# One hybrid-decoder layer on one core: the tokens' own part computed in the scan's head, with the inverse's second product and with kappa

## The chip, the core and the metric

The kernel runs on one core of one Trainium2 chip. The core has a matrix engine (TensorE, PE in the profile; its weight loads are shown as PEld), VectorE (DVE), ScalarE (ACT), GpSimd (POOL) and a queue engine for DMAs (SyncE, SP). The time is device microseconds of one execution. The kernel before takes 1354.36 us, the median of three runs (1353.73 to 1357.92).

## What is computed

One inference step of one layer: RWKV-7 time mixing beside dilated sliding-window attention, gated and merged, for a prompt of 1024 tokens and 8 short samples. Only the RWKV part of the prompt matters here. Per head it is a recurrence over tokens on a 64x64 state S:

```python
def step(S, inp):
    r_t, w_t, k_t, v_t, kk_t, a_t = inp
    sa = jnp.einsum('bhvk,bhk->bhv', S, -kk_t)
    S = (S * w_t[:, :, None, :] + sa[..., None] * (kk_t * a_t)[:, :, None, :]
         + v_t[..., None] * k_t[:, :, None, :])
    return S, jnp.einsum('bhvk,bhk->bhv', S, r_t)

S_fin, o = lax.scan(step, wkv0.astype(F32), xs)
```

## The kernel before

The recurrence is done in chunks of 64 tokens. Inside a chunk the removal terms `sa` of the 64 tokens depend on each other through a triangular matrix; its inverse is needed. A *unit* is one pair of heads (j = 0..3) and one half of the prompt (hf = 0, 1): 8 units, each with 8 chunks. Five streams of work share the core in the first stage of the kernel, up to about 615 us:

- `products`: the input projection, 36 blocks of 128 columns in this stage (`project_steps`, line L178). One piece is four matmuls of 128x352, written to a bank `pj`. This is the bulk of PE's work and it can go between anything.
- `units` (generator `unit`): prepares a unit on DVE and ACT, with small matmuls: the normalisation (L326), the decay and rate gates (L306), the transpose of the norms (L349; after it on DVE the block L351, L353, L357, L359, L360 of 128x512 operations), the triangular products (L385) with their masks on DVE (L392, into `AT`), the bonus (L405), transposes of v (L413, into `W`) and of the keys (L423, into `BT`), and last **R0** (L432): 16 matmuls of 64x64 of `AT` and `W`, moved out of PSUM by ACT at L436. R0 is the tokens' own part: what the values of a chunk's own tokens give to its removal terms.
- `inverses` (`inverse`): two 32x32 blocks of each triangle are inverted on DVE by forward substitution, `tm` and `X` (L457, L460, 62 operations a unit), after a DMA to DRAM and back (`Yd`, `Y`); the result goes back to `AT` by DMA through `Xd` (L464).
- `scans` (`scan`): the scan of a unit. Its *head* joins the two 32x32 inverses into a 64x64 one: DMAs `AT<-Xd` and a transpose `T1` on DVE (L479), a transpose of kappa (L484), the first product `pm` (L492), the second product `pg` (L502), moved into `AT` by ACT (L508). Then kappa is multiplied by the inverse (L518, banks `pk`, moved into `KR` by ACT at L523), and R0 is multiplied by the inverse (L528, bank `pu`, moved back into `R0` by ACT at L532). Then 8 *hops*, one a chunk: `KR` with the state (L543), W on DVE (L544), `BT` with W (L549), the new state on DVE (L552). Last the outputs (L560).
- `norms` (`norm`): the group norm of a finished scan (DVE, ACT, and the transposes L589).

PE executes in the order in which the program is written; DVE, ACT and the queues are ordered by the framework's scheduler. The written order comes from a planner, `run_streams`: each stream yields a pair, the PE time of what it has just written and the delay after which its next step is due. Whenever a stream is due its step is written; otherwise a piece of projection is. `own` streams (scans and inverses) go ahead of the limit on small work, the others wait while more than `SMALL` of it is owed. PSUM banks go round by name: `sc` has two, `g` has two, `pj` has four.

Of the kernel before, what the change touches and what calls it, by code (L numbers as in the profile page):

```python
# [14 lines left out]
AF = mybir.ActivationFunctionType  # L15
# [3 lines left out]
P = 128  # L19
# [12 lines left out]
D_PN, D_KR, D_AT, D_G, D_W, D_INV, D_UP = 0.65, 1.81, 4.5, 0.2, 2.09, 1.3, 8.4  # L32
D_PM, D_HOP, D_ST, D_GN, D_IN, D_U0, D_MASK = 0.9, 1.25, 1.75, 12.6, 11.0, 1.2, 1.2
# [51 lines left out]
def tile_layer(ctx: ExitStack, tc: tile.TileContext, A: dict, O: list):  # L85
    nc = tc.nc
    V, S, G, T, SP = nc.vector, nc.scalar, nc.gpsimd, nc.tensor, nc.sync
# [29 lines left out]
    rp = rw_stack.enter_context(tc.tile_pool(name="rp", bufs=1))  # L117
# [199 lines left out]
    def unit(j, hf, M, st, out):  # L317
# [47 lines left out]
        E = mk(rp, [P, 8, 65], "E", 2)  # L365
# [3 lines left out]
        KR = mk(rp, [P, 4, 4, 64], "KR", 2)  # L369
# [8 lines left out]
        AT = mk(rp, [P, 2, 8, P], "AT", 2)  # L378
        for h in range(2):
            pA = [ps("g") for e in range(2)]  # L380
            for q in range(4):
                c = 4 * h + q
                for e in range(2):
# [5 lines left out]
                        start=True, stop=True,  # L389
# [13 lines left out]
        bon = t_("bon", 2)  # L403
# [6 lines left out]
        W = mk(rp, [P, 8, P], "W", 2)  # L410
# [7 lines left out]
        BT = mk(rp, [P, 8, P], "BT", 2)  # L418
        for h in range(2):
# [3 lines left out]
                T.transpose(pt[:, q * P : (q + 1) * P], BK[:, c // 2, 2 * (c % 2) : 2 * (c % 2) + 2, :], ident)  # L423
            S.activation(BT[:, 4 * h : 4 * h + 4, :], pt.rearrange("p (a b) -> p a b", a=4), AF.Copy)
            yield (0.45, D_W)
        R0 = mk(rp, [P, 4, P], "R0", 2)
        pr = ps("g")
        for c2 in range(4):
            for e in range(2):
                for p in range(2):  # L430
                    u, v = slice(64 * (1 - p), 64 * (1 - p) + 64), slice(64 * p, 64 * p + 64)
                    T.matmul(  # L432
                        pr[u, c2 * P + 64 * e : c2 * P + 64 * e + 64], AT[v, e, 2 * c2 + p, u], W[v, 2 * c2 + p, 64 * e : 64 * e + 64],
                        start=True, stop=True,
                    )
        S.activation(R0[:], pr.rearrange("p (a b) -> p a b", a=4), AF.Copy)  # L436
        yield (1.0, D_G)

        out.append((j, hf, KR, AT, W, BT, R0, E, bon, st))


    def inverse(j, hf, AT, out):
# [25 lines left out]
        out.append((Xd, blk))  # L468


    def scan(j, hf, KR, AT, W, BT, R0, E, bon, st, Xd, blk, out):

        T1 = mk(rp, [P, 8, 32], "T1", 1)
        quads = [(p, 64 * (1 - p), n, n // 4, 2 * (n % 4) + p) for p in range(2) for n in range(8)]
        for p in range(2):
            u = 64 * (1 - p)
# [5 lines left out]
        pk = ps("sc")  # L482
# [3 lines left out]
        for p in range(2):  # L486
            u, v = slice(64 * (1 - p), 64 * (1 - p) + 64), slice(64 * p, 64 * p + 64)
# [3 lines left out]
        for _, u, n, e, c in both:  # L491
            T.matmul(  # L492
                pm[u + 32 : u + 64, 32 * n : 32 * n + 32], AT[u : u + 32, e, c, u + 32 : u + 64], T1[u : u + 32, n, :],
                start=True, stop=True,
            )
        for p in range(2):
            u = 64 * (1 - p)
# [3 lines left out]
        for _, u, n, e, c in both:  # L501
            T.matmul(  # L502
                pg[u : u + 32, 32 * n : 32 * n + 32], T1[u + 32 : u + 64, n, :], AT[u + 32 : u + 64, e, c, u + 32 : u + 64],
                start=True, stop=True,
            )
        for p in range(2):
            u = 64 * (1 - p)
            S.activation(  # L508
                AT[u : u + 32, :, p::2, u + 32 : u + 64], pg[u : u + 32, 0:256].rearrange("p (a b c) -> p a b c", a=2, b=4), AF.Copy
            )  # L510
        yield (0.6, D_PM)


        chunks = [(c // 2, c % 2, e) for c2 in range(4) for e in range(2) for c in (2 * c2, 2 * c2 + 1)]
        pk = [ps("sc") for p in range(2)]
        for c2, p, e in chunks:
            u = slice(64 * (1 - p), 64 * (1 - p) + 64)
# [1 line left out]
                pk[p][64 * e : 64 * e + 64, 64 * c2 : 64 * c2 + 64],  # L519
                kT[u, c2, 64 * e : 64 * e + 64], AT[u, e, 2 * c2 + p, u], start=True, stop=True,  # L520
            )
        for p in range(2):
            S.activation(KR[:, :, 1 + p, :], pk[p][:, 0:256].rearrange("p (a b) -> p a b", a=4), AF.Copy, scale=-1.0)  # L523
        yield (1.0, D_PM)
        pu = ps("sc")
        for c2, p, e in chunks:
            u = slice(64 * (1 - p), 64 * (1 - p) + 64)
            T.matmul(  # L528
                pu[u, c2 * P + 64 * e : c2 * P + 64 * e + 64],
                AT[u, e, 2 * c2 + p, u], R0[u, c2, 64 * e : 64 * e + 64], start=True, stop=True,  # L530
            )
        S.activation(R0[:], pu.rearrange("p (a b) -> p a b", a=4), AF.Copy, scale=-1.0)  # L532
        yield (1.0, D_U0)

        Ot = mk(rp, [P, 4, P], "Ot", 2)
        for c in range(8):
            p, c2 = c % 2, c // 2
            u, v = slice(64 * (1 - p), 64 * (1 - p) + 64), slice(64 * p, 64 * p + 64)
# [3 lines left out]
            pr = ps("sc")  # L542
# [14 lines left out]
        for c in range(8):  # L557
            c2, v = c // 2, slice(64 * (c % 2), 64 * (c % 2) + 64)
# [39 lines left out]
    def state_out(j, st):  # L598
        b = ps("g")
        T.transpose(b[:, 0:P], st[0][:], ident)  # L600
        so = mk(rp, [P, P], "so", 1)
        S.activation(so[:], b[:, 0:P], AF.Copy)
        for e in range(2):
            d = slice(64 * e, 64 * e + 64)
            S.dma_start(O[8][0, 0, 2 * j + e], so[d, d])
# [878 lines left out]
```

## Time and profile before

| what | value |
|---|---|
| median of 3 runs | 1354.36 us |
| the profiled execution | 1353.07 us, of which the span from first to last instruction is 1351.2 us |
| PE busy | 1318.8 us, 98% of the span |
| DVE, ACT, POOL busy | 805.1, 469.3, 67.6 us |
| first stage, 76 to 600 us | 524 us, of which PE busy 510.26 us |
| R0 (L432) and its product with the inverse (L528) on PE | 9.2 us busy each, in 8 units |

PE's busy time counts overlapping matmuls once, and the end of a matmul is modelled, so a small idle time hides part of a loss. A better measure of what a group costs PE is the distance from its start to the start of the next group. In the timeline rows of the prediction the columns are the start in us, the time to the end of the row's last instruction, engine, line, operation, output and inputs, forms, count; a wait in brackets is idle time ahead of it with what ended it. fp32 matmuls stand twice in the profile's counts (32 for the 16 of R0).

### The profile page before, as it was taken

What the parts mean: (1) busy time and instruction counts of PE and PEld (TensorE: products, weight loads), DVE (VectorE), ACT (ScalarE), POOL (GpSimd) and SP (SyncE); (2) the same over time, 40 slices, a digit from 0 to 9 for tenths busy, and PEclk for the clock granted to TensorE, in tenths of its full rate; (3) what the DMA queues carried; (4) which work ended last, traced back from release to release, by engine and by line L of the source; (5) the groups of instructions that cost most, each with busy time, mean ns of one, the idle gap of its engine ahead of it and who ended that gap; (6) DMA issues with size and microseconds to landing.
All of it is one profiled execution on the core that took longest, in us unless ns stands there. A gap on an engine that the chain in (4) does not pass through costs nothing.

```text
span 1351.2 us, 25749 instructions
## 1 busy us (share of the span) xinstructions
PE 1318.8 (98%) x10005; PEld 1238.6 (92%) x10005; DVE 805.1 (60%) x2204; ACT 469.3 (35%) x1065; POOL 67.6 (5%) x82
## 2 busy tenths in 40 slices
PE   9999999999999999999999999999999998999997
PEld 7998999898988999999999999999999997899786
DVE  5677668686576856552554376437544744655565
ACT  5334344434344443422332333232333234132211
POOL 0000000000000000000000000000000000025100
PEclk9999999999999999999999999999999999999999
DMA  6122223222313242326646365545555566795221
GB/s 211 45 60 64 71 87 88 62 58 78 100 53 87 81 112 85 93 92 135 134 104 134 98 144 113 127 119 122 113 128 134 123 134 164 219 298 166 91 98 66
DMA packets 340151, 151.64 MB, mean 112 GB/s; under 512 B 188808, under 2 KB 329502, under 8 KB 339774
## 3 DMA queue, kind: packets, MB, share of 16 engines
q1 hardware_dynamic: 241150, 129.68, 35.3%
q10 hardware_dynamic: 98880, 20.32, 7.6%
q8 instruction: 79, 1.29, 0.4%
q14 instruction: 42, 0.34, 0.1%
HBM read 110.68 MB, written 38.97 MB: 111 GB/s over the span
## 4 chain that ended last, share of the span: by engine, by line
PE 82%; DVE 11%; DMA 3%; issue 1%; ACT 1%; SPq 0%; POOL 0%; ACTq 0%; DVEq 0%; POOLq 0%
PE pj L178 60%; PE pj L1438 7%; PE s L948 2%; PE o L985 2%; DMA kc<-in_cache_kv_g_dram 2%; DVE tm L457 2%; DVE X L460 2%; PE g L385 1%; PE t L968 1%; DVE st L552 1%; PE sc L543 1%; DVE wlo L169 1%; PE sc L549 1%; DMA cb<-yd 1%; PE sc L528 1%
## 5 line engine op out<-in xcount | busy, mean ns | idle before, releaser
L178 PE MATMUL pj<-xhi,whi 128*128 128x352 f32 x1848 | 396.4, 336 | 4.3 <-ACT xhi L1305 2.9
L178 PE MATMUL pj<-xhi,wlo 128*128 128x352 f32 x1848 | 385.7, 330 | 0.0
L178 PE MATMUL pj<-xlo,whi 128*128 128x352 f32 x1848 | 381.1, 327 | 0.0
L178 PEld LDWEIGHTS pj<-xhi,whi 128*128 128x128 f32 x1848 | 305.3, 190 | 14.4 <-issue 4.4
L178 PEld LDWEIGHTS pj<-xlo,whi 128*128 128x128 f32 x1848 | 309.4, 190 | 2.3 <-issue 1.3
L178 PEld LDWEIGHTS pj<-xhi,wlo 128*128 128x128 f32 x1848 | 307.8, 190 | 3.7 <-issue 1.9
L169 DVE TENSOR_TENSOR wlo<-wraw,whi 128x512 fp32r<-128x512 f32 x162 | 113.9, 704 | 74.4 <-ACT whi L168 73.9
L168 ACT ACTIVATE whi<-wraw 128x512 fp32r<-128x512 f32 x162 | 100.5, 625 | 117.1 <-PE pj L178 73.4
L958 ACT ACTIVATE Sm<-Sm,nm 128x128 f32<-128x128 f32 (+1 forms) x96 | 42.4, 442 | 88.4 <-DVE nm L955 88.4
L457 DVE TENSOR_TENSOR tm<-Y,X 128x60 f32<-128x60 f32 (+24 forms) x248 | 52.0, 210 | 10.7 <-DMA Y<-Yd 4.4
L950 DVE CUSTOM_DVE_ANT_0 Sm<-s,cst 128x128 f32<-128x128 f32 (+1 forms) x96 | 29.2, 347 | 45.5 <-PE s L948 45.4
L460 DVE TENSOR_TENSOR X<-X,tm 128x60 f32<-128x60 f32 (+24 forms) x248 | 51.8, 209 | 6.0
L552 DVE SCALAR_TENSOR_TENSOR st<-sc,E,SD 64x64 f32<-64x64 f32 x128 | 36.1, 282 | 29.5 <-PE sc L549 27.8
L1438 PE MATMUL pj<-wl,mh 128*128 128x512 f32 (+1 forms) x136 | 52.0, 382 | 0.0
L541 ACT ACTIVATE SD<-st,E 128x128 f32<-128x128 f32 x64 | 25.7, 401 | 70.9 <-DVE st L552 70.8
L811 POOL TENSOR_TENSOR kvp<-vv,kv 128x512 f32<-128x512 f32 x16 | 21.2, 1331 | 461.0 <-DVE Ss L819 376.5
L985 PE MATMUL o<-PT,Vt 128*128 128x128 f32 x280 | 38.6, 275 | 0.8 <-ACT PT L972 0.8
L985 PEld LDWEIGHTS o<-PT,Vt 128*128 128x128 f32 x280 | 36.6, 191 | 1.3 <-ACT PT L972 1.1
L948 PE MATMUL s<-k,q 128*128 128x128 f32 (+1 forms) x192 | 37.7, 325 | 0.1
L873 ACT ACTIVATE k<-pj 128x352 f32<-128x352 f32 (+1 forms) x36 | 16.3, 456 | 61.6 <-PE pj L178 56.8
L311 ACT ACTIVATE zt<-pj,der 128x352 f32<-128x352 f32 x48 | 26.5, 552 | 31.7 <-PE pj L178 26.4
L873 ACT ACTIVATE q<-pj 128x352 f32<-128x352 f32 (+1 forms) x36 | 16.4, 455 | 58.4 <-PE pj L178 54.6
(325 smaller groups left out, 1687.3 us busy)
## 6 DMA issues: line engine op xcount, KB each, us to landing
wraw<-in_w_in_dram SPq DMA_DIRECT2D x146, 256.0 KB
gd<-zt SPq DMA_DIRECT2D x48, 176.0 KB
gt<-gd SPq DMA_DIRECT2D x48, 176.0 KB
vs<-bt ACTq DMA_DIRECT2D x48, 128.0 KB
kc<-in_cache_kv_g_dram SPq DMA_DIRECT2D x48, 128.0 KB
Vt<-vs ACTq DMA_DIRECT2D x12, 512.0 KB
cb<-cd SPq DMA_DIRECT2D x12, 512.0 KB
zd<-zt SPq DMA_DIRECT2D x24, 176.0 KB
```

The costliest lines, as they stand in the source:

```text
L168: S.activation(hi[:], raw[:], AF.Copy)
L169: V.tensor_tensor(lo[:], raw[:], hi.bitcast(F32)[:], ALU.subtract)
L178: T.matmul(out, w[wi][:, n % 4, :], x[:, n % 4, :], start=first and n == 0, stop=last and n == 11)
L457: V.tensor_tensor(tm, Y[:, r : r + 1, r + 1 : 32].to_broadcast([P, m, n]), X[:, 0:m, r : r + 1].to_broadcast([P, m, n]), ALU.mult)
L460: V.tensor_tensor(X[:, 0:m, r + 1 : 32], X[:, 0:m, r + 1 : 32], tm, ALU.subtract)
L552: V.scalar_tensor_tensor(S1[d, d], pS[d, d], E[d, c, 64:65], SD[d, d], ALU.mult, ALU.add)
L873: S.activation(classes(dst[:], d)[:, :, t0 // d : (t0 + n) // d], b[:, 0:n].rearrange("p (i c) -> p c i", c=d), AF.Copy)
L948: T.matmul(r, qT[:, i * P : (i + 1) * P], kT[:, keys[i][0] * P : keys[i][0] * P + n], start=True, stop=True)
L950: V.tensor_tensor_reduce(out=Sm[:, i, 0:n], in0=r, in1=m3 if g == 2 else m12[:, 256 - n : 256], scale=1.0, scalar=NEG, op0=ALU.add, op1=AL ...
L958: S.activation(Sm[:, i, 0:n], Sm[:, i, 0:n], AF.Exp, scale=SCALE, bias=nm[:, x : x + 1], accum_out=ml[:, g, 1, i : i + 1])
L985: T.matmul(po[:, (i % 4) * P : (i % 4 + 1) * P], st["Vt"][:, kb_, :], PT[:, n * P : (n + 1) * P], start=m == 0, stop=m == len(keys[i]) - 1,)
L1438: T.matmul(pb[:], a[:, k], wk, start=x == 0, stop=x == len(prods) - 1)
```

## The change

R0's 16 matmuls leave `unit` and stand in `scan`, directly behind the second product `pg`; their bank is still a `g`. R0's eviction stands behind the two of `pg`. R0 has one buffer where it had two. The product of R0 with the inverse (`pu`) is written directly behind kappa's (`pk`), ahead of kappa's evictions, and its bank is a `g` where it was an `sc`. The planner is told 1.2 for `pg` with R0 (0.6 before), 1.7 for `pk` with `pu` (1.0 and 1.0 before, as two steps), and one step of 1.0 fewer in `unit`. No DMA moves, and the number of instructions that compute is the same.

```diff
@@ unit
-        R0 = mk(rp, [P, 4, P], "R0", 2)
-        pr = ps("g")
-        for c2 in range(4):
...
-        S.activation(R0[:], pr.rearrange("p (a b) -> p a b", a=4), AF.Copy)
-        yield (1.0, D_G)
@@ scan
+        R0 = mk(rp, [P, 4, P], "R0", 1)
+        pr = ps("g")
+        for c2 in range(4):
+            for e in range(2):
+                for p in range(2):
+                    u, v = slice(64 * (1 - p), 64 * (1 - p) + 64), slice(64 * p, 64 * p + 64)
+                    T.matmul(
+                        pr[u, c2 * P + 64 * e : c2 * P + 64 * e + 64], AT[v, e, 2 * c2 + p, u], W[v, 2 * c2 + p, 64 * e : 64 * e + 64],
+                        start=True, stop=True,
+                    )
         for p in range(2):
             u = 64 * (1 - p)
             S.activation(
                 AT[u : u + 32, :, p::2, u + 32 : u + 64], pg[u : u + 32, 0:256].rearrange("p (a b c) -> p a b c", a=2, b=4), AF.Copy
             )
-        yield (0.6, D_PM)
+        S.activation(R0[:], pr.rearrange("p (a b) -> p a b", a=4), AF.Copy)
+        yield (1.2, D_PM)
...
-        for p in range(2):
-            S.activation(KR[:, :, 1 + p, :], pk[p][:, 0:256].rearrange("p (a b) -> p a b", a=4), AF.Copy, scale=-1.0)
-        yield (1.0, D_PM)
-        pu = ps("sc")
+        pu = ps("g")
         for c2, p, e in chunks:
...
+        for p in range(2):
+            S.activation(KR[:, :, 1 + p, :], pk[p][:, 0:256].rearrange("p (a b) -> p a b", a=4), AF.Copy, scale=-1.0)
         S.activation(R0[:], pu.rearrange("p (a b) -> p a b", a=4), AF.Copy, scale=-1.0)
-        yield (1.0, D_U0)
+        yield (1.7, D_U0)
```

**Place 1, PE in the head of the second scan.** In the rows a name's number tells one tile from another; L178 is a piece of projection. Before, from the first product (L492) to the first of kappa's matmuls (L518):

```order
L492 MATMUL sc_2210<-T_391_2191,AT_1114 32x32 x16
L178 MATMUL pj_2025<-xlo_13_94,whi_2124 128x352 x4
L178 MATMUL pj_2238<-xhi_10_91,whi_2243 128x352 x4
L502 MATMUL sc_2251<-AT_1114,T_391_2191 32x32 x16
L178 MATMUL pj_2238<-xhi_10_91,wlo_2244 128x352 x4
L178 MATMUL pj_2238<-xlo_12_93,whi_2243 128x352 x4
L518 MATMUL sc_2278<-AT_1114,sz_2203 64x64
```

Before, from the last of kappa's matmuls to the first hop (L543):

```order
L518 MATMUL sc_2279<-AT_1114,sz_2203 64x64
L178 MATMUL pj_2239<-xhi_10_91,whi_2243 128x352 x4
L589 MATMUL g_2302<-ident_69,Ot_1574 128x128 x4
L528 MATMUL sc_2313<-R_237_1303,AT_1114 64x64 x16
L178 MATMUL pj_2239<-xhi_10_91,wlo_2244 128x352 x4
L178 MATMUL pj_2239<-xlo_12_93,whi_2243 128x352 x4
L405 MATMUL g_2340<-t_2104,cst_76 128x512
L543 MATMUL sc_2346<-st_67_385,KR_1053 128x128
```

Now the same two stretches (L479 is the first product, L489 the second, L500 is R0, L517 kappa, L524 `pu`, L541 the hop, L587 the norm's transposes):

```order
L479 MATMUL sc_2213<-T_391_2185,AT_1079 32x32 x16
L178 MATMUL pj_2200<-xhi_10_91,wlo_2206 128x352 x4
L178 MATMUL pj_2200<-xlo_12_93,whi_2205 128x352 x4
L489 MATMUL sc_2240<-AT_1079,T_391_2185 32x32 x16
L500 MATMUL g_2258<-W_1176,AT_1079 64x64 x16
L178 MATMUL pj_2201<-xhi_10_91,whi_2205 128x352 x4
L587 MATMUL g_2282<-ident_69,Ot_1569 128x128 x4
L517 MATMUL sc_2293<-AT_1079,sz_2197 64x64
```

```order
L517 MATMUL sc_2294<-AT_1079,sz_2197 64x64
L524 MATMUL g_2311<-R_402_2257,AT_1079 64x64 x16
L178 MATMUL pj_2201<-xhi_10_91,wlo_2206 128x352 x4
L178 MATMUL pj_2201<-xlo_12_93,whi_2205 128x352 x4
L178 MATMUL pj_2202<-xhi_10_91,whi_2205 128x352 x4
L541 MATMUL sc_2346<-st_67_385,KR_1024 128x128
```

R0 has joined the second product and `pu` has joined kappa, with no piece between; one piece and the norm's transposes stand between R0 and kappa.

**Place 2, DVE at the head of the first scan.** T1 is the transpose that the first product waits for (L479, now L466); the 128x512 rows at L351 to L360 prepare the third unit, and the rows at L242 to L253 shift a projected block `m`. Before:

```order
L351 SCALAR_TENSOR_TENSOR t_1414<-m_789,prm_96,g_1409 128x512
L479 STREAM_TRANSPOSE T_258_1425<-AT_704 32x256
L353 SCALAR_TENSOR_TENSOR t_1416<-t_1382,t_1414 128x512
L359 SCALAR_TENSOR_TENSOR BK_1422<-t_1416,t_1387 128x4x128
L357 TENSOR_TENSOR t_1420<-m_789,t_1418 128x512
L479 STREAM_TRANSPOSE T_258_1425<-AT_704 32x256
L360 TENSOR_TENSOR BK_1422<-t_1420,t_1387 128x4x2x64
```

Now:

```order
L353 SCALAR_TENSOR_TENSOR t_1370<-t_1333,t_1368 128x512
L359 SCALAR_TENSOR_TENSOR BK_1376<-t_1370,t_1338 128x4x128
L357 TENSOR_TENSOR t_1374<-m_789,t_1372 128x512
L242 SCALAR_TENSOR_TENSOR m_1210<-pj_1214,prm_96,m_1210 128x319
L360 TENSOR_TENSOR BK_1376<-t_1374,t_1338 128x4x2x64
L244 SCALAR_TENSOR_TENSOR m_1210<-lst_1211,prm_96,m_1210 128x1
L251 SCALAR_TENSOR_TENSOR sM_99<-pj_1214,prm_96,sM_99 128x8x3
L252 SCALAR_TENSOR_TENSOR sM_99<-shT_98,prm_96,sM_99 128x8
L253 COPY zl_100<-pj_1214 128x9
L466 STREAM_TRANSPOSE T_262_1421<-AT_704 32x256 x2
```

Both transposes now stand behind the whole block. On PE the scan's head comes later against the preparation: L349 and L484 stood in one visit, and now six pieces stand between L349 and L471.

**Place 3, DVE between the hops of the second scan**, where the same block meets the hops' operations (W at L544, now L542; the state at L552, now L550; L460 and L457, now L447 and L444, are the next unit's inverse). Before:

```order
L552 SCALAR_TENSOR_TENSOR st_67_385<-sc_2601,E_1050,SD_2568 64x64
L343 SCALAR_TENSOR_TENSOR t_2589<-cst_76,t_2584 128x512
L552 SCALAR_TENSOR_TENSOR st_67_385<-sc_2601,E_1050,SD_2568 64x64
L351 SCALAR_TENSOR_TENSOR t_2620<-m_789,prm_96,g_2615 128x512
L460 TENSOR_TENSOR X_2421<-X_2421,tm_2638 128x4x16
L353 SCALAR_TENSOR_TENSOR t_2622<-t_2586,t_2620 128x512
L457 TENSOR_TENSOR tm_2655<-Y_2416,X_2421 128x75
L359 SCALAR_TENSOR_TENSOR BK_2628<-t_2622,t_2591 128x4x128
L357 TENSOR_TENSOR t_2626<-m_789,t_2624 128x512
L544 TENSOR_TENSOR W_1205<-sc_2647,R_237_1303 64x128
```

Now:

```order
L343 SCALAR_TENSOR_TENSOR t_2572<-cst_76,t_2567 128x512
L550 SCALAR_TENSOR_TENSOR st_67_385<-sc_2584,E_1021,SD_2551 64x64 x2
L444 TENSOR_TENSOR tm_2665<-Y_2428,X_2433 128x75
L351 SCALAR_TENSOR_TENSOR t_2603<-m_789,prm_96,g_2598 128x512
L447 TENSOR_TENSOR X_2433<-X_2433,tm_2665 128x5x15
L353 SCALAR_TENSOR_TENSOR t_2605<-t_2569,t_2603 128x512
L542 TENSOR_TENSOR W_1176<-sc_2630,R_402_2257 64x128
L357 TENSOR_TENSOR t_2609<-m_789,t_2607 128x512
L359 SCALAR_TENSOR_TENSOR BK_2611<-t_2605,t_2574 128x4x128
L360 TENSOR_TENSOR BK_2611<-t_2609,t_2574 128x4x2x64
L444 TENSOR_TENSOR tm_2668<-Y_2428,X_2433 128x70
L550 SCALAR_TENSOR_TENSOR st_68_386<-sc_2661,E_1021,SD_2628 64x64 x2
```

Both halves of the state now stand behind L343, and W stands two 128x512 operations earlier. Behind the first stage the order is the same on PE from the last scan's end on.

More of the change, by code (lines that the diff above doesn't have):

```diff
@@ L425, in unit @@
             yield (0.45, D_W)
-        R0 = mk(rp, [P, 4, P], "R0", 2)
-        pr = ps("g")
-        for c2 in range(4):
-            for e in range(2):
-                for p in range(2):
[L431 to L436, printed above, removed]
-        yield (1.0, D_G)
-        out.append((j, hf, KR, AT, W, BT, R0, E, bon, st))
+        out.append((j, hf, KR, AT, W, BT, E, bon, st))
     def inverse(j, hf, AT, out):
@@ L468, in inverse, with scan @@
         out.append((Xd, blk))
-    def scan(j, hf, KR, AT, W, BT, R0, E, bon, st, Xd, blk, out):
+    def scan(j, hf, KR, AT, W, BT, E, bon, st, Xd, blk, out):
         T1 = mk(rp, [P, 8, 32], "T1", 1)
@@ L521, in scan @@
             )
-        for p in range(2):
-            S.activation(KR[:, :, 1 + p, :], pk[p][:, 0:256].rearrange("p (a b) -> p a b", a=4), AF.Copy, scale=-1.0)
-        yield (1.0, D_PM)
-        pu = ps("sc")
+        pu = ps("g")
         for c2, p, e in chunks:
@@ L731, in scans @@
             if args[1]:
-                state_out(args[0], args[9])
+                state_out(args[0], args[8])
                 yield 0.1, 0.0
```

## The prediction

> **What bounds the kernel now.** I read the page first, for the engine that bounds, then the busy times by stretch, then PE's waits, then the timeline of PE and DVE where the change is.
>
> ```profile
> PE 1318.8 (98%) x10005; PEld 1238.6 (92%) x10005; DVE 805.1 (60%) x2204; ACT 469.3 (35%) x1065; POOL 67.6 (5%) x82
> 76.00:600.00 524.00, 510.26 (x4568) 479.60 (x4567) 354.85 (x1215) 217.65 (x471) 5.92 (x20) 0.99 0.28 79
> ```
>
> The second row is the first stage: its length, then the busy time of PE, PEld, DVE, ACT, POOL, then the granted clock. PE is idle for 13.7 us of 524, so the stage is as long as PE's work in it: a step off PE's path is worth nothing, and a step that only changes place on PE is worth what the place costs. Pieces of projection are left when the last scan ends, in the new order too, so that nothing runs bare at the stage's end, and behind it PE's order is unchanged. The sum therefore has two kinds of term: what a visit between pieces costs PE beside its matmuls, and PE's waits.
>
> ```profile
> PE sc L543 <- DVE st L552: 7.0, 8, 2.2
> PE sc L492 <- DVE T L479: 3.3, 3, 2.1
> PE sc L549 <- DVE W L544: 2.3, 3, 1.1
> PE g L385 <- DVE BK L360: 0.5, 1, 0.5
> PE g L385 <- DVE AT L392: 0.3, 1, 0.3
> ```
>
> These are all of PE's waits between 60 and 600 us (total, times, longest): 13.4 us, and each ends with DVE. None is for R0, for kappa or for their evictions.
>
> **The change, part by part.** *Joined visits.* The price of a visit is read from the third scan's head:
>
> ```profile
> 235.02 1.16 PE L385 MATMUL g<-KR,BK 64*128 64x128 f32 x16
> 236.11 0.69 PE L492 MATMUL sc<-T,AT 32*32 32x32 f32 x32
> ...
> 239.69 1.16 PE L385 MATMUL g<-KR,BK 64*128 64x128 f32 x16
> 240.79 0.69 PE L518 MATMUL sc<-AT,sz 64*64 64x64 f32 x32
> 241.41 0.92 PE L178 MATMUL pj<-xhi,wlo 128*128 128x352 f32 x4
> 242.17 0.81 PE L178 MATMUL pj<-xlo,whi 128*128 128x352 f32 x4
> 242.91 1.15 PE L528 MATMUL sc<-R,AT 64*64 64x64 f32 x32
> 243.99 0.91 PE L178 MATMUL pj<-xhi,whi 128*128 128x352 f32 x4
> ...
> 489.25 0.81 PE L178 MATMUL pj<-xhi,wlo 128*128 128x352 f32 x4
> ...
> 490.54 0.81 PE L178 MATMUL pj<-xhi,whi 128*128 128x352 f32 x4
> ```
>
> In a plain run two pieces go by in 1.29 us (489.25 to 490.54). Between two groups that use part of the array (L518 and L528) two pieces take 1.50 us (241.41 to 242.91). So leaving such a group and entering the next costs 0.21 us beside the matmuls. Where two stand together it is not paid: L385 takes 1.09 to 1.10 us to the next start whether 32x32 (L492) or 64x64 matmuls (L518) follow. In the order, PE has 69 such blocks of part-array groups before and 57 after: 16 joints are made (R0 to `pg`, `pu` to kappa, in 8 scans) and 4 are lost (two masks' products with kappa, two with the first product, which no longer coincide). 12 x 0.21 = **-2.5 us**. Bounds: 16 x 0.21 = -3.4 if the lost joints cost nothing, 0 if a joint of these kinds saves nothing. I take the middle one, because the four lost joints are in the row above as savings. A group of 128x128 matmuls (transposes, hops) that a visit loses or gains I cost at nothing: R0 left hops, whose own cost is paid alone or in company.
>
> *Evictions.* R0's and `pu`'s on ACT are as many as before:
>
> ```profile
> L436 ACT ACTIVATE R<-g x8: 577/590/600, 78.1 to 507.3; 128x512 f32<-128x512 f32 x8
> L508 ACT ACTIVATE AT<-sc x16: 372/374/377, 125.1 to 559.1; 32x256 f32<-32x256 f32 x16
> ```
>
> The two of `pg` (0.75 us) now run beside R0's 1.08 us of matmuls, and R0's 0.59 us beside a piece, the norm's transposes and kappa's 0.62 us: about 1.8 us of cover. Behind it on ACT wait the norm's eviction and kappa's two, which the hop needs three pieces later. I take 0; if other ACT work comes between, the cover is short by at most one 0.6 us operation, +5 us in 8 scans. `pu` in `g` no longer waits for kappa's eviction but for R0's, which it needs anyway. The single R0 buffer is free since the previous scan's last W, over ten pieces earlier. No DMA and no queue is touched.
>
> *The first scan's head.* Here stands the largest wait of the stretch:
>
> ```profile
> 118.39 0.24 PE L492 MATMUL sc<-T,AT 32*32 32x32 f32 x2 [0.23 <-DVE T L479]
> 120.78 0.95 PE L492 MATMUL sc<-T,AT 32*32 32x32 f32 x30 [2.15 <-DVE T L479]
> 121.66 1.54 PE L178 MATMUL pj<-xhi,whi 128*128 128x352 f32 x4
> ...
> 124.31 0.71 PE L502 MATMUL sc<-AT,T 32*32 32x32 f32 x32
> 118.37 0.69 DVE L353 SCALAR_TENSOR_TENSOR t<-t,t 128x512 f32<-128x512 f32 x1
> ...
> 119.70 0.68 DVE L357 TENSOR_TENSOR t<-m,t 128x512 f32<-128x512 f32 x1
> 120.30 0.43 DVE L479 STREAM_TRANSPOSE T<-AT 32x256 f32<-32x256 f32 x1
> ...
> 121.23 0.53 DVE L242 SCALAR_TENSOR_TENSOR m<-pj,prm,m 128x319 f32<-128x319 f32 x1
> ...
> 123.05 0.22 DVE L252 SCALAR_TENSOR_TENSOR sM<-shT,prm,sM 128x8 f32<-128x8 f32 x1
> ```
>
> The second transpose stands on DVE behind three operations of the third unit. With two R0 visits fewer ahead, that unit's norms are six pieces (3.9 us) ahead of the scan's head. The whole block is then ahead of the transposes: five operations of 0.69, two shifts of 0.53, six small ones of about 0.2 and two transposes of 0.43, 6.6 us if nothing overlaps. The first product comes seven pieces of 0.645 us and kappa's transposes after L349, about 5.0 us. So I let 1.2 us of wait stay (between the 1.6 of this count and nothing, since rows on DVE start up to 0.1 before the last one's end). The 2.4 us of idle time in the rows (0.23 and 2.15) are 3.1 us by starts: the first product takes 3.27 us to the next start (118.39 to 121.66), where the third scan's takes about 0.62 (0.69 less the overlap), and began late. **-1.9 us**, bounds -3.1 and +1.
>
> After that wait eight matmuls of projection take 2.65 us (121.66 to 124.31) where two pieces take 1.29:
>
> ```profile
> 116.00:126.00 10.00, 7.62 (x95) 6.71 (x94) 8.98 (x28) 5.02 (x12) 0.00 (x0) 0.83 0.18 52
> 270.46 0.46 PE L543 MATMUL sc<-st,KR 128*128 128x128 f32 x2 [1.35 <-DVE st L552]
> ...
> 332.42 0.61 PE L543 MATMUL sc<-st,KR 128*128 128x128 f32 x2 [2.25 <-DVE st L552]
> 332.68 1.52 PE L178 MATMUL pj<-xhi,whi 128*128 128x352 f32 x4
> ```
>
> The granted clock of that stretch is 0.83, and the same slow matmuls follow the only other wait of over 2 us, at 332; after the one of 1.35 us they don't. With the wait down to 1.2 us I take the slow pieces away: **-1.4 us**, bounds -1.4 and 0. The Trainium skill (TensorE: Matmul & The Clock Gate, Part 1) has the clock fall to half after an idle window of about 3.4 us. By that alone 2.15 us would not do it and this term would be 0, the sum 1350.1; the trace shows the fall at 2.15, and it decides.
>
> *The other scans.* Most of the remaining waits come where the block L351 to L360 meets the hops:
>
> ```profile
> 206.89 1.21 DVE L343 TENSOR_TENSOR_SCAN t<-cst,t 128x512 f32<-128x512 f32 x1
> 208.13 0.29 DVE L552 SCALAR_TENSOR_TENSOR st<-sc,E,SD 64x64 f32<-64x64 f32 x1
> ...
> 210.72 0.69 DVE L357 TENSOR_TENSOR t<-m,t 128x512 f32<-128x512 f32 x1
> 211.44 0.29 DVE L544 TENSOR_TENSOR W<-sc,R 64x128 f32<-64x128 f32 x1
> ...
> 211.79 0.49 PE L549 MATMUL sc<-W,BT 128*128 128x128 f32 x2 [0.83 <-DVE W L544]
> ```
>
> In the new order both state updates are behind L343 (0.3 later), W is two operations earlier (1.3), and the next state update is behind those two (0.6 later than due). In two of the five scans with such a block, the shifts of a projected block stand in it as well, some 1.5 us more. Gains and losses cancel by these prices, and I take **0** for scans two to eight, bounds -9 (all of these waits go) and +9 (they double).
>
> Sum: -2.5 - 1.9 - 1.4 = -5.8 us against the profiled execution, 1353.07, its span 1351.2 and 1.9 around it: 1347.3. That execution is 1.3 us under the median of the runs shown, so the median after comes to 1354.36 - 5.8 = **1348.6 us**. No change and a change of under 0.3% (4.1 us) can't be told apart by measurement.
>
> **The rivals.** *Only the joints pay.* The waits are set by the order on DVE, and the first scan's goes elsewhere, since DVE is busy for 8.98 of the 10 us around it. Then -2.5: 1351.9, no change. For it: every wait row is DVE's. Against: six pieces of distance are more than the block's length.
>
> *Slower: the transposes hold the masks.* In five of the later scans T1 stands on DVE ahead of the masks of the next unit, and waits there for a DMA:
>
> ```profile
> 484.96 0.44 DVE L479 STREAM_TRANSPOSE T<-AT 32x256 f32<-32x256 f32 x1 [0.18 <-DMA AT<-Xd]
> 485.43 1.29 DVE L392 TENSOR_TENSOR AT<-g,cst 128x512 f32<-128x512 f32 x2
> 486.18 1.74 PE L385 MATMUL g<-KR,BK 64*128 64x128 f32 x16
> ```
>
> There 0.18 us of wait for the DMA made L385 take 1.74 us, 0.58 over the 1.16 above. If the DMA lands 2 us late against the masks, it is 2.4 us a scan, 12 in five: 1354.4 - 5.8 + 12 = 1360.6. It decides from 2 us a scan on (10 us against 5.8). Against it: the inverse ends during the seventh hop in the new order, over ten pieces ahead of the masks.
>
> *R0's eviction is late.* `pu` waits for it, 0.6 us in 8 scans: 1353.4, no change.
>
> *Joints are not free.* The Trainium skill (TensorEngine Tiling (Array Packing), Key Properties) says that a change of tiling mode drains the engine. `pg` (32x32) to R0 (64x64) is such a change. As a mechanism here: if that joint paid the whole 0.21, 8 x 0.21 = 1.7 us come back, 1350.3, at the edge of no change. The row at 235.02 speaks against it: 1.09 us ahead of 32x32 matmuls.
>
> **How the numbers follow.** Forecast 0.56; only the joints 0.23; R0 late 0.09; joints not free 0.05; slower by the transposes 0.07. The forecast is over 0.3% faster, the next three are within it: 0.56, 0.37, 0.07. The range reaches down by half of the later waits (4.5 us, 1344) and up to no change of the median (1354.5); beyond lie the slow rival and the full gain.
>
> **What would show it.** Right: `pg` with R0, and kappa with `pu`, without a piece between, 1.7 us each from start to next start; PE's waits for T1 at 1.5 us or less in all; no clock of 0.83 around 120 us. Wrong: a wait of `pu` for the eviction of R0, a wait of L385 for the masks in most scans, waits for the hops' DVE work of over 13 us, or a wait of over 2 us anywhere new, which brings slow pieces with it.

## The result, and the profile after

The changed kernel takes 1344.08 us (median of 6 runs, 1342.51 to 1347.45) beside 1355.43 us before on the same chip: ratio 0.9926, 95% interval 0.9913 to 0.9939. In a second comparison it came to 0.9925 (0.991 to 0.994). The two medians lie 11.4 us apart, and by its ratio the kernel is faster by 10.0 us. The prediction had 1348.6 with a range of 1344.0 to 1354.5 and a gain of 5.8: the side is right, the time stands at the very end of the range, and the gain is 1.7 to 2 times what was forecast. The profiled execution has a span of 1341.8 us, 9.4 less than before.

The page's busy times:

```profile
PE 1312.3 (98%) x10005; PEld 1233.8 (92%) x10005; DVE 804.8 (60%) x2204; ACT 469.0 (35%) x1065; POOL 68.7 (5%) x82
```

The same two stretches of the first stage as were shown of before (length, then busy time of PE, PEld, DVE, ACT, POOL, granted clock):

```profile
76.00:600.00 524.00, 514.26 (x4663) 485.76 (x4662) 362.79 (x1236) 220.49 (x477) 6.69 (x20) 1.00 0.28 80
116.00:126.00 10.00, 9.26 (x177) 8.24 (x177) 9.21 (x34) 5.34 (x12) 0.00 (x0) 1.00 0.27 78
```

In the 524 us that started alike, PE does 4663 matmuls instead of 4568. In the ten microseconds around the first scan's head it does 177 instead of 95 (32 of them are R0's small ones, which stood elsewhere before), and the granted clock is 1.00 where it was 0.83. PE's waits between 60 and 610 us (total, times, longest), all of them:

```profile
PE sc L541 <- DVE st L550: 4.5, 10, 0.9
PE sc L547 <- DVE W L542: 3.8, 3, 2.0
PE sc L479 <- DVE T L466: 0.7, 2, 0.5
PE g L385 <- DVE BK L360: 0.5, 1, 0.5
```

They are 9.5 us instead of 13.4. L541 and L547 are the hops (L543 and L549 before), L479 is the first product that waits for T1 (L492 before): its wait fell from 3.3 to 0.7, the hops' from 9.3 to 8.3. The first scan's head on PE, with the two new visits:

```profile
119.34 0.24 PE L479 MATMUL sc<-T,AT 32*32 32x32 f32 x2 [0.52 <-DVE T L466]
119.81 0.69 PE L479 MATMUL sc<-T,AT 32*32 32x32 f32 x30 [0.22 <-DVE T L466]
...
121.89 0.69 PE L489 MATMUL sc<-AT,T 32*32 32x32 f32 x32
122.51 1.15 PE L500 MATMUL g<-W,AT 64*64 64x64 f32 x32
123.59 0.91 PE L178 MATMUL pj<-xhi,whi 128*128 128x352 f32 x4
```

The second product (L489) and R0 (L500) take 1.70 us from start to next start (121.89 to 123.59), with no piece and no wait between. The gain is made in the first stage: PE's last transposes of a norm stand at 613.86 us before and at 603.03 after, -10.8; of these 1.4 are given back later.

### The profile page after: what moved, and what is told of

It is laid out like the page before. It is cut to its first block, busy times and chain, and to the rows that moved or that the text cites. A ratio compares the mean times of both kernels' runs of the same rounds, so it can differ in the third digit from the quotient of the medians.

```text
span 1341.8 us, 25749 instructions
## 1 busy us (share of the span) xinstructions
PE 1312.3 (98%) x10005; PEld 1233.8 (92%) x10005; DVE 804.8 (60%) x2204; ACT 469.0 (35%) x1065; POOL 68.7 (5%) x82
## 4 chain that ended last, share of the span: by engine, by line
PE 80%; DVE 13%; DMA 4%; issue 2%; ACT 1%; SPq 0%; ACTq 0%; DVEq 0%
PE pj L178 58%; PE pj L1436 7%; DVE tm L444 2%; DVE X L447 2%; PE s L946 2%; PE o L983 2%; DMA kc<-in_cache_kv_g_dram 1%; PE g L385 1%; DVE st L550 1%; PE t L966 1%; DVE wlo L169 1%; PE sc L541 1%; DMA cb<-yd 1%; PE sc L547 1%; DMA wraw<-in_w_in_dram 1%
## 5 line engine op out<-in xcount | busy, mean ns | idle before, releaser
L178 PE MATMUL pj<-xhi,whi 128*128 128x352 f32 x1848 | 396.1, 335 | 4.5 <-ACT xhi L1303 2.7
L178 PE MATMUL pj<-xhi,wlo 128*128 128x352 f32 x1848 | 381.9, 328 | 0.0
L178 PE MATMUL pj<-xlo,whi 128*128 128x352 f32 x1848 | 381.2, 327 | 0.0
L178 PEld LDWEIGHTS pj<-xhi,whi 128*128 128x128 f32 x1848 | 303.7, 189 | 16.2 <-issue 5.4
L178 PEld LDWEIGHTS pj<-xlo,whi 128*128 128x128 f32 x1848 | 308.5, 189 | 1.4 <-issue 0.6
L178 PEld LDWEIGHTS pj<-xhi,wlo 128*128 128x128 f32 x1848 | 307.2, 189 | 1.9 <-issue 0.9
L447 DVE TENSOR_TENSOR X<-X,tm 128x60 f32<-128x60 f32 (+24 forms) x248 | 52.1, 210 | 6.4
L444 DVE TENSOR_TENSOR tm<-Y,X 128x60 f32<-128x60 f32 (+24 forms) x248 | 52.0, 210 | 6.0
L550 DVE SCALAR_TENSOR_TENSOR st<-sc,E,SD 64x64 f32<-64x64 f32 x128 | 36.0, 282 | 18.3 <-PE sc L547 16.9
L543 ACT ACTIVATE Ot<-sc 64x128 f32<-64x128 f32 x64 | 17.4, 271 | 60.3 <-DVE W L542 60.2
L542 DVE TENSOR_TENSOR W<-sc,R 64x128 f32<-64x128 f32 x64 | 18.4, 288 | 30.9 <-PE sc L541 24.7
```

The costliest lines, as they stand in the source:

```text
L178: T.matmul(out, w[wi][:, n % 4, :], x[:, n % 4, :], start=first and n == 0, stop=last and n == 11)
L444: V.tensor_tensor(tm, Y[:, r : r + 1, r + 1 : 32].to_broadcast([P, m, n]), X[:, 0:m, r : r + 1].to_broadcast([P, m, n]), ALU.mult)
L447: V.tensor_tensor(X[:, 0:m, r + 1 : 32], X[:, 0:m, r + 1 : 32], tm, ALU.subtract)
L550: V.scalar_tensor_tensor(S1[d, d], pS[d, d], E[d, c, 64:65], SD[d, d], ALU.mult, ALU.add)
```

## The experiments

Counted in the order of instructions, PE has 60 blocks of part-array groups before and 48 after (the prediction counted 69 and 57, with another end of the stage; the difference of 12 is the same). All runs together; "waits" are all of PE's waits between 60 and 610 us in the profiled execution, "half clock" the stretches of 3.4 us at half the granted clock in the first stage of that execution:

| kernel | ratio to before, 95% interval | blocks | waits, us | half clock |
|---|---|---|---|---|
| before | 1 | 60 | 13.4 | 2 |
| changed | 0.9926 (0.9913 to 0.9939) | 48 | 9.5 | 0 |
| only R0 moved | 1.0027 (1.0015 to 1.0039) | 53 | 17.1 | 2 |
| only kappa and `pu` joined | 0.9936 (0.9921 to 0.9951) | 54 | 10.7 | 1 |
| changed, a piece between | 0.9902 (0.9885 to 0.9919) | 56 | 6.5 | 0 |
| changed, costs told as before | 0.9990 (0.9977 to 1.0002) | 45 | 13.7 | 1 |
| changed, two operations on GpSimd | 1.0015 (1.0003 to 1.0027) | 48 | 19.2 | 2 |
| before, `pu` told 0.7 | 0.9955 (0.9940 to 0.9971) | 64 | 11.1 | 0 |
| changed, told 1.4 | 0.9956 (0.9942 to 0.9971) | 48 | 10.8 | 2 |
| before, two operations on GpSimd | 1.0028 (1.0019 to 1.0037) | 60 | 17.7 | 0 |
| before, R0 told 0.4 | 0.9983 (0.9970 to 0.9996) | 64 | 10.3 | 1 |
| changed, again | 0.9925 (0.9910 to 0.9940) | 48 | 9.1 | 1 |
| a piece between, again | 0.9912 (0.9896 to 0.9929) | 56 | 6.4 | 0 |

**Theory and rivals at the start.** The gain is a sum: joined visits (about 3.4 us), the first scan's head with its slow pieces (about 3.5), and the rest from the order that the later scans came to have on PE and DVE. Rivals: only the joints pay; one half of the edit gives everything; the later scans wait less because R0 has left the preparation. The first two runs make each half of the edit alone.

Only R0 moved:

```
-        pu = ps("g")
+        for p in range(2):
+            S.activation(KR[:, :, 1 + p, :], pk[p][:, 0:256].rearrange("p (a b) -> p a b", a=4), AF.Copy, scale=-1.0)
+        yield (1.0, D_PM)
+        pu = ps("sc")
...
-        for p in range(2):
-            S.activation(KR[:, :, 1 + p, :], pk[p][:, 0:256].rearrange("p (a b) -> p a b", a=4), AF.Copy, scale=-1.0)
...
-        yield (1.7, D_U0)
+        yield (1.0, D_U0)
```

> The changed kernel, but the second use of the inverse (the tokens' own part, pu) has a visit of its own again, behind kappa's evictions and in the bank it had before; so only R0's move is left. Blocks of part-array groups: 60 before, 48 changed, 53 here (counted in the order of TensorE's instructions). Theory (joined visits + first scan's head + a better order in the later scans, each with its own price): the first head is as in the changed kernel (pm waits about 1 us for T1, no half clock around 121 us: -2.1 and -1.4), the visits give 7 x 0.21 = -1.5, the later scans are newly ordered and may give anything from -3 to +3: about 1350.4 where before has 1355.4, ratio 0.9963 (0.994 to 0.9985). Rival 'only the joined visits pay': ratio 0.9989. Rival 'the move of R0 is the whole gain': 0.9926, as the changed kernel.

It came out slower than before, 1.0027. Its first head is the changed kernel's, the row for T1 is the same; but the hops wait 15.1 us (its lines are one further down):

```profile
PE sc L548 <- DVE W L543: 9.7, 7, 2.3
PE sc L542 <- DVE st L551: 5.4, 6, 2.4
PE sc L479 <- DVE T L466: 0.7, 2, 0.5
```

One of these waits in its timeline (start, duration):

```profile
207.90 0.69 DVE L353 SCALAR_TENSOR_TENSOR t<-t,t 128x512 f32<-128x512 f32 x1
...
208.70 0.69 DVE L359 SCALAR_TENSOR_TENSOR BK<-t,t 128x512 f32<-128x512 f32 x1
209.31 0.69 DVE L357 TENSOR_TENSOR t<-m,t 128x512 f32<-128x512 f32 x1
...
210.03 0.69 DVE L360 TENSOR_TENSOR BK<-t,t 128x512 f32<-128x512 f32 x1
...
210.76 0.28 DVE L543 TENSOR_TENSOR W<-sc,R 64x128 f32<-64x128 f32 x1
...
211.09 0.49 PE L548 MATMUL sc<-W,BT 128*128 128x128 f32 x2 [2.28 <-DVE W L543]
```

The hop's W stands on DVE behind four 128x512 operations of the preparation. So the head's gain was there, but the later scans lost more than it. None of the three expected ratios held. The later scans took about 8 us more than before's (the other waits 16.4 us against 10.1, and one half clock more), where I allowed 3.

Only kappa and `pu` joined, R0 left in the preparation (the kernel before; `pu`'s bank is a `g` as in the changed kernel, not one of kappa's, as the expectation has it):

```
-        for p in range(2):
-            S.activation(KR[:, :, 1 + p, :], pk[p][:, 0:256].rearrange("p (a b) -> p a b", a=4), AF.Copy, scale=-1.0)
-        yield (1.0, D_PM)
-        pu = ps("sc")
+        pu = ps("g")
...
+        for p in range(2):
+            S.activation(KR[:, :, 1 + p, :], pk[p][:, 0:256].rearrange("p (a b) -> p a b", a=4), AF.Copy, scale=-1.0)
...
-        yield (1.0, D_U0)
+        yield (1.7, D_U0)
```

> The kernel before, R0 in the preparation, with kappa and pu in one visit (pu in kappa's bank rotation, the planner told 1.7). Blocks of part-array groups: 54 against 60 before. Theory: the first head is as before (pm waits 3.1 us for T1, the half clock around 121 us stays), the visits give 6 x 0.21 = -1.3, and the joint of kappa and pu by its own price (0.14 more each, 8 times) another -1.1: -2.4 us and what the new order of later scans brings (-3 to +3), ratio 0.9982 (0.996 to 1.0005). Rival 'the second half is the whole gain': 0.9926.

0.9936, -8.7 us: far more than the -2.4 us of its joints, and outside of what was expected. T1's wait is there as expected, and so is the half clock behind it; the hops wait 7.5 us, and the half clock at 332 us is gone:

```profile
PE sc L548 <- DVE W L543: 5.2, 5, 1.7
PE sc L492 <- DVE T L479: 2.4, 2, 2.1
PE sc L542 <- DVE st L551: 2.3, 3, 0.9
```

**The joint's price.** In the changed kernel, a piece can stand between kappa's matmuls and those of `pu`:

```
+        yield (0.8, 0.3)
         pu = ps("g")
...
-        yield (1.7, D_U0)
+        yield (0.9, D_U0)
```

> The changed kernel with the visit of kappa and pu cut in two, so that a projection piece can stand between them; same places, banks and evictions behind both. Blocks 56 against 48 of the changed kernel, the order otherwise nearly the same. Theory: eight more block ends at 0.21 to 0.35 us: 1.7 to 2.8 us longer than the changed kernel, ratio to before 0.9939 to 0.9947, waits and clock as in the changed kernel. Rival 'joints are free, the gain is in waits': as the changed kernel, 0.9926 +- 0.0005.

The price is there, row by row. First the changed kernel's second head, then this one's:

```profile
182.74 0.69 PE L517 MATMUL sc<-AT,sz 64*64 64x64 f32 x32
183.26 1.10 PE L524 MATMUL g<-R,AT 64*64 64x64 f32 x32
184.29 0.92 PE L178 MATMUL pj<-xhi,wlo 128*128 128x352 f32 x4
...
186.33 0.38 PE L541 MATMUL sc<-st,KR 128*128 128x128 f32 x2
```

```profile
182.55 0.69 PE L517 MATMUL sc<-AT,sz 64*64 64x64 f32 x32
183.18 0.91 PE L178 MATMUL pj<-xlo,whi 128*128 128x352 f32 x4
184.02 1.15 PE L525 MATMUL g<-R,AT 64*64 64x64 f32 x32
...
186.49 0.81 PE L178 MATMUL pj<-xlo,whi 128*128 128x352 f32 x4
```

Kappa, `pu` and three pieces take 3.59 us joined (182.74 to 186.33). Kappa, a piece, `pu` and two pieces take 3.94 cut (182.55 to 186.49 is the start of the third piece). So a cut costs 0.35 us (the starts in the other heads differ from these by 0.03 us at most), 2.8 in eight scans, the upper end of what was expected. But the kernel is not longer: 0.9902, below both expected ratios. Its hops wait less by 3.0 us than the changed kernel's (8.3 there):

```profile
PE sc L542 <- DVE st L551: 4.4, 10, 0.9
PE sc L548 <- DVE W L543: 0.9, 4, 0.3
```

The cost was paid and given back by an order in which no wait for W is over 0.3 us. To see whether the cut gains, both kernels ran again, side by side.

> The changed kernel itself, beside the next one on the same chip: ratio to before 0.9926 as first measured (0.9913 to 0.9939).

> The kernel with a piece between kappa and the tokens' own part, again, to tell whether cutting the joined visit costs or gains over the changed kernel. Theory (eight block ends cost 1.6 us in visits, and the other order of the later scans gives back 1.7 us of hop waits): same as the changed kernel within 0.1%, ratio 0.992 to 0.993. Rival 'the cut itself gains': 0.9902 as in its first runs, 2 to 3 us ahead of the changed kernel.

1344.5 us for the changed kernel (1344.27 to 1347.54) and 1343.24 with the cut (1341.87 to 1345.19); ratios 0.9925 and 0.9912, with intervals that overlap. The cut is ahead both times, by 0.13% to 0.24%; that it is faster is likely and not shown.

**Only the told costs.** In the changed kernel the planner is told what before's visits came to, 1.6 for 1.2 and 2.0 for 1.7; no instruction is other:

```
-        yield (1.2, D_PM)
+        yield (1.6, D_PM)
...
-        yield (1.7, D_U0)
+        yield (2.0, D_U0)
```

> The changed kernel; only the planner's two told costs are larger (1.6 for 1.2, and 2.0 for 1.7, the totals of the visits they came from), so that pieces and later scans come in another order; the first scan's head stands in the same place. Blocks 45 against 48. Theory (the gain beyond joints and first head is the order that the planner happened on): waits of the hops return to 11 us or more from 8.3 and a drop of the clock may come back: 1 to 5 us longer than the changed kernel, ratio to before 0.9933 to 0.9963; the first head is as in the changed kernel. Rival 'moving R0 out of the preparation itself makes the later scans wait less': as the changed kernel, 0.992 to 0.993.

0.9990: nearly all of the gain is gone, more than either expectation allowed, with every joint and the new place of the first head kept.

```profile
PE sc L547 <- DVE W L542: 6.1, 4, 2.8
PE sc L541 <- DVE st L550: 3.3, 5, 1.6
PE g L385 <- DVE AT L392: 1.0, 2, 0.7
PE sc L479 <- DVE T L466: 0.7, 2, 0.5
```

Waits of ten kinds add up to 13.7 us. A half clock stands behind one of 2.14 us at 328 us; behind the longest, 2.75 us at 398, there is none. The second stage loses as well, 4.2 us against before from the first stage's end: 2.4 in the wait of L1149 for its DMA and a half clock from 779 us on. The rival that R0's leaving the preparation makes the later scans wait less falls.

**A new theory.** The order of PE showed that before's heads stand 71, 60, 71, 64, 60, 71 and 68 pieces apart, the changed kernel's 69, then 64 five times, and 70: one pattern for every scan. The smaller told total would be what lets the planner repeat a pattern, and the repeated pattern waits less. Three runs change one told number each. `pu` in the kernel before:

```
-        yield (1.0, D_U0)
+        yield (0.7, D_U0)
```

> The kernel before with one number changed: the planner is told 0.7 for the tokens' own part in place of 1.0. No instruction is added, removed or joined. By the order of TensorE's instructions, the scans' heads then stand 71, 63, 63, 63, 63, 63, 67 pieces apart (before 71, 60, 71, 64, 60, 71, 68; changed 69, 64, 64, 64, 64, 64, 70), so that the scans come in one and the same pattern; blocks of part-array groups 64 against 60. New theory, after the first four runs (most of the gain is that the smaller told total lets the planner repeat one pattern, in which the hops wait less): pm's wait of 3.1 us and the half clock at 121 us stay; the other waits fall by 4, the half clock at 332 us goes (-1.7), four blocks cost 0.8: about -5 us, ratio 0.9963 (0.994 to 0.998). Rival 'the gain needs the change's own edits (joined visits, later head)': 1.0006 +- 0.001.

The joined visit in the changed kernel:

```
-        yield (1.7, D_U0)
+        yield (1.4, D_U0)
```

> The changed kernel with one number changed: the joined visit of kappa and the tokens' own part is told as 1.4 in place of 1.7. Heads of scans are then 69, 62, 62, 62, 62, 62, 70 pieces apart (changed: 64 each), blocks 48 as there. New theory: one pattern for all scans again, so about as fast as the changed kernel, ratio to before 0.9926 (0.990 to 0.995). Rival 'the changed kernel's 64 is a lucky distance, any other order waits as the four unlucky ones did': 0.997 or more.

R0 in the kernel before:

```
-        yield (1.0, D_G)
+        yield (0.4, D_G)
```

> The kernel before with one number changed: the planner is told 0.4 in place of 1.0 for R0's visit in the preparation. No instruction is added, removed or joined. By TensorE's order the first scan's head then stands at piece 132 as in the changed kernel (before 128), and the later heads 71, 63, 63, 63, 63, 63, 69 pieces apart; blocks of part-array groups 64 against 60 of before. Theory (first head by its place alone; one pattern for all scans as in the run with 0.7 told, which was -6.1 us): pm's wait for T1 falls from 2.7 there to about 1, no half clock around 121 us, the rest as there: -7 to -8 us, ratio 0.9945 (0.992 to 0.997). Rival 'the first head needs R0 out of the preparation': pm waits 3 us again, ratio 0.9955 or more.

The first gave 0.9955, as the theory had it: one number, no other edit, and over half of the change's gain. The second, the changed kernel in another even pattern, gave 0.9956, between theory and rival: it is 4 us behind the changed kernel, with two half clocks after waits of 2.1 and 2.0 us at 271 and 390 us. The third gave 0.9983, outside of the theory's range. Its head came as predicted from its place alone (T1's wait 1.4 us, no half clock around 121), with R0 still in the preparation; but two hops waited over 2 us:

```profile
PE sc L549 <- DVE W L544: 4.6, 3, 2.2
PE sc L543 <- DVE st L552: 4.3, 13, 0.8
PE sc L492 <- DVE T L479: 1.4, 2, 1.2
```

So most of the early wait hangs on the head's place, not on where R0 is computed, and the told costs decide the later scans. That an even pattern is what makes them wait less is not shown: of five even orders, two (with the cut, `pu` told 0.7) have no hop's wait over 1.7 us, the changed kernel has one of 1.99, and two (told 1.4, R0 told 0.4) have two of 2.0 to 2.2. And the kernel with only kappa and `pu` joined, whose heads stand 69, 65, 55, 68, 55, 68 and 65 pieces apart, is nearly as fast as the changed one, with a longest hop's wait of 1.7 us. What a long wait is made of can be read: in the traces of the kernels with nothing moved to GpSimd, hops wait 13 times for 1.98 us or more, and in 11 of these waits DVE does L357, L359 and L360 of the preparation, as in the timeline above. A rule by which a told number leads to such a meeting was not found.

**The block on GpSimd.** Two of its five 128x512 operations, L357 and L360, move from VectorE to GpSimd, in the changed kernel and in the kernel before:

```
-        V.tensor_tensor(k2[:], Mk[:, sl], f2[:], ALU.mult)
+        G.tensor_tensor(k2[:], Mk[:, sl], f2[:], ALU.mult)
...
-        V.tensor_tensor(BK[:, :, 0:4:3, :], c2p(k2), c2p(Ei), ALU.mult)
+        G.tensor_tensor(BK[:, :, 0:4:3, :], c2p(k2), c2p(Ei), ALU.mult)
```

> The changed kernel with two of the five 128x512 operations of the preparation (k2 and BK's outer half, L357 and L360) on GpSimd in place of VectorE; TensorE's order is word for word the changed kernel's. Theory (a hop waits because one to three of these operations, 0.7 us each, stand just ahead of its own on VectorE): the hops' waits on TensorE, 8.3 us in the changed kernel from 60 to 610 us, fall to 5 or less, ratio to before 0.990 to 0.9915. Rival 'the hops wait for the path through TensorE and ScalarE, whatever stands on VectorE': waits and time as in the changed kernel (0.9926). Rival 'GpSimd is late and the grams wait for BK': L385 waits for GpSimd by over 2 us, 0.994 or more.

> The kernel before, its order untouched, with the same two operations on GpSimd (L357, L360). Theory (those operations, where they stand ahead of a hop's, make the waits): the hops' waits, 9.3 us from 60 to 610 us, fall to 5 or less, the 2.2 us wait at 332 us with its half clock goes: -3 to -6 us, ratio 0.9955 to 0.998. Rival 'VectorE's load is not the cause': 1.000 +- 0.001.

Both theories fell: 1.0015 and 1.0028, slower than before. In the kernel before, the long waits did go, with both half clocks (longest hop wait 1.5 us), but more short ones came, 12.8 us in all:

```profile
PE sc L543 <- DVE st L552: 10.9, 16, 1.5
PE sc L549 <- DVE W L544: 1.9, 4, 0.6
```

Its timeline shows one of them:

```profile
212.42 1.79 POOL L357 TENSOR_TENSOR t<-m,t 128x512 f32<-128x512 f32 x1 [44.78 <-DVE tm L457]
...
214.24 1.90 DVE L373 SCALAR_TENSOR_TENSOR t<-m,prm,t 128x512 f32<-128x512 f32 x1
214.28 1.30 POOL L360 TENSOR_TENSOR BK<-t,t 128x512 f32<-128x512 f32 x1
...
216.57 0.58 DVE L552 SCALAR_TENSOR_TENSOR st<-sc,E,SD 64x64 f32<-64x64 f32 x2
...
217.30 0.46 PE L543 MATMUL sc<-st,KR 128*128 128x128 f32 x2 [1.42 <-DVE st L552]
```

L373 on DVE takes 1.90 us while GpSimd works on L360, and the hop's state update comes behind it. By groups, L373 and L359 of this kernel, then of the kernel before (busy time, mean ns):

```profile
L373 DVE SCALAR_TENSOR_TENSOR t<-m,prm,t 128x512 f32<-128x512 f32 x8 | 9.4, 1170 | 1.2 <-POOL t L357 1.2
L359 DVE SCALAR_TENSOR_TENSOR BK<-t,t 128x512 f32<-128x512 f32 x8 | 8.4, 1048 | 0.1
```

```profile
L373 DVE SCALAR_TENSOR_TENSOR t<-m,prm,t 128x512 f32<-128x512 f32 x8 | 5.9, 744 | 0.0
L359 DVE SCALAR_TENSOR_TENSOR BK<-t,t 128x512 f32<-128x512 f32 x8 | 5.5, 686 | 0.0
```

DVE lost 16 operations of 0.68 us and is busy 4.6 us longer (809.7 us against 805.1). Besides these two groups (6.4 us longer together) L460 and L370 are longer, by 4.3 and 2.2 us. The Trainium skill (SBUF — State Buffer, Who interferes with whom) says that VectorE and GpSimd share one pair of ports, locked for one of them at a time, and that a VectorE operation with two inputs in SBUF contends with a GpSimd operation that reads there. These rows agree: all four groups have two such inputs. By that rule the move had to cost something, which neither expectation counted. So the two runs don't tell what the hops would wait if the block cost DVE nothing. They do show what DVE alone can do: in the changed kernel the pieces between the heads are the same with and without the move, and by the ratios the move made it 12 us longer, beside 9.7 us more of waits and two half clocks.

**Does the table add up?** Take 0.21 us for a block, 0.14 more for each of eight cuts between kappa and `pu` (0.35 by the rows above), 1.65 for a half clock (3.4 us at half the rate lose 1.6 to 1.7), and the waits as they are, all against before. The changed kernel comes to -3.9 - 3.3 - 2.5 - 1.1 = -10.8 us, measured -10.0 by its ratio. For the other runs, in the table's order, computed and measured: +2.2 and +3.7, -6.7 and -8.7, -11.0 and -13.3, -5.6 and -1.4, +2.2 and +2.0, -4.8 and -6.1, -6.2 and -6.0, +1.0 and +3.8, -3.9 and -2.3, -9.6 and -10.2, -11.1 and -11.9. All but one agree within 3 us; the one, off by 4.2, is the run whose second stage lost 4.2. Waits and half clocks run from 6.4 to 22.5 us over these kernels, the visits over 5: the order on DVE weighs more than what was edited. But waits and half clocks are those of one execution each, and half clocks come and go between executions: of before's, the ten with a mean clock of 0.992 took 1355.9 us in the mean, the fourteen with 0.995 took 1353.4. The mean clock of 59 executions of before is 0.9931, of 11 of the changed kernel 0.9948, which is about 1.3 half clocks fewer (0.0017 x 1350 us by 1.7, an estimate) and not the two of the profiled executions.

## Why the prediction was right, and where its sum was off

*The bound* was read rightly. PE's work, its waits and its clock in the first stage account for the times of all kernels but one to within 3 us. *The time* is inside the range by 0.1 us, and that is luck: the range was built on before's 1354.36, and from the 1355.43 of the comparison it would begin at 1345.1. What the forecast had right is the side and three of its terms; the gain is well over its sum, for the reasons below.

*Joined visits, -2.5.* The count of blocks held (12 fewer). The price of 0.21 was too small for one kind: kappa with `pu` saves 0.35. That makes 2.5 + 8 x 0.14 = 3.6 us, beyond the bound of 3.4. So kappa with `pu` takes 1.55 us from start to next start (182.74 to 184.29), where 1.7 was said. The 0.21 from the rows of before is what the two pieces between lose; that the two groups themselves run closer was not counted. Apart, L518 and L528 take 0.62 and 1.08 us to the next start; joined, L517 and L524 take 0.52 and 1.03. No price shows between the second product and R0: L489 takes 0.62 us to L500's start (121.89 to 122.51), and before, ahead of a piece, the second product of the third scan took 0.63 (L502, 238.22 to 238.85).

*Evictions, 0.* Right: no row of PE's waits names an eviction of R0, AT or KR.

*The first head, -1.9.* T1's wait fell by 2.6 us in the wait rows; by starts the first product takes 1.08 us (119.34 to 120.42) instead of 3.27, which is -2.2. The 1.2 us that I let stay were 0.7. The reason given, two visits of R0 fewer, was only the way there. The head's place four pieces later was enough for most of it: the kernel with R0 told 0.4 has both visits and a wait of 1.4.

*Slow pieces, -1.4.* Gone in every kernel with the later head. But the term is what one execution of before paid: the kernel with `pu` told 0.7 keeps the wait of 2.15 us and has no half clock behind it (last section). What the step left out is the second, behind the 2.25 us wait at 332 us: another -1.65 in the profiled execution. (The sum without this term is 1348.6 + 1.4 = 1350.0, not 1350.1.)

*The other scans, 0 with bounds of 9.* For the changed kernel the hops' waits fell by 1.0 us and the long one at 332 went, with its half clock: with the wait of the masks (0.3) about -3 in all. This is the step that was mis-sized, with the joints' 1.1. Its bounds held, and they were most of the uncertainty: with the same edits, one told number moved this term from about -3 to +1.7 (told 1.4), and two to +2.9 in the first stage; with `pu` apart again it was about +8. My estimate of a few operations at a few places could not have found the side.

*The rivals.* Only the joints pay: not so. Transposes that hold the masks: no wait of L385 for them is left in the rows after. R0's eviction late, joints not free: neither is in the rows. The one that was missing: the new order lets the hops meet the preparation's block more often, as it did with only R0 moved (1.0027) and with the costs told as before (0.9990). The changed kernel came near to a sign of being wrong itself, a new wait of over 2 us: it has one of 1.99 us at 271 us.

## What to carry to other kernels

Where a planner fills one engine's order from told costs, an edit changes two things: the work, and where everything behind it falls. Price the first from rows, and find the second by trying neighbouring told costs: here one number was worth -6 us without any edit, and one number took back 4 of the change's 10. Before work is moved to another engine to relieve the one that is waited for, look for what the two share.

## What the runs showed of the hardware that was not expected

The half clock does not follow the length of the wait alone. The same wait of 2.15 us for T1 stands in the kernel before (the prediction's rows at 120.78) and in the one with `pu` told 0.7, whose clock in the same ten microseconds is 1.00 and not 0.83:

```profile
121.12 0.69 PE L492 MATMUL sc<-T,AT 32*32 32x32 f32 x30 [2.15 <-DVE T L479]
```

And one kernel, the changed one, had a wait of 1.99 us at 271 us without it in one execution and one of 1.98 with it in another. The two rows are the same stretch of the two executions, the clock the last number but two (the first run, then the run again):

```profile
272.50:276.50 4.00, 4.00 (x28) 4.00 (x27) 3.65 (x15) 1.92 (x4) 0.00 (x0) 1.00 0.23 66
```

```profile
272.50:276.50 4.00, 4.00 (x18) 4.00 (x17) 3.11 (x14) 1.29 (x3) 0.00 (x0) 0.57 0.23 66
```

Ten matmuls fewer at 0.161 us are the 1.6 us that such a stretch costs.

What decides, in these traces, is where the wait falls. In all thirteen traces the clock changes only at whole multiples of 3.413 us from the first entry of the trace's clock record. Cut at these points, the first stages (60 to 615 us) make 2099 stretches. In twelve of them PE is busy for 1.50 us or less, and each of the twelve has a half clock behind it; in all others PE is busy for 1.56 us or more, and none has. In the kernel before, the wait for T1 lies in one stretch, and the next one is at half the clock:

```profile
117.55:120.96 3.41, 1.03 (x16) 0.62 (x16) 3.31 (x7) 2.94 (x5) 0.00 (x0) 1.00 0.00 0
120.96:124.38 3.42, 3.42 (x40) 2.97 (x36) 3.08 (x12) 1.04 (x3) 0.00 (x0) 0.50 0.16 44
```

With `pu` told 0.7 the same wait lies across an end at 119.89:

```profile
116.48:119.89 3.41, 2.26 (x18) 1.84 (x16) 3.11 (x7) 1.96 (x5) 0.00 (x0) 1.00 0.29 86
119.89:123.31 3.42, 2.19 (x43) 1.93 (x44) 3.38 (x11) 2.01 (x5) 0.00 (x0) 1.00 0.00 0
```

So it is with the 2.75 us wait at 398 us, which an end at 396.49 divides, and with the changed kernel's wait at 271 us: the stretch that holds most of it is busy for 1.71 us in the one execution and for 1.44 in the other. Where the ends lie differs from one execution to the next. An estimate from these figures: a wait of 2.15 us alone, if the ends fell at random, would leave a stretch with 1.50 us or less in (3.41 - 2.15 + 2 x 0.24) / 3.41, about half of the executions, and a single wait under 1.9 us in none. The 1.50 us hold for this stage alone: behind it, stretches with up to 2.06 us of busy PE have a half clock behind them.
